# A decoder trunk's first mixer, its pieces put on TensorE in an order written out by hand

## The chip, the core and the metric

The kernel runs on one core of one Trainium2 chip. TensorE (PE in the profile) multiplies matrices and also transposes tiles by multiplying them with an identity. VectorE (DVE), ScalarE (ACT) and GpSimd (POOL) do the elementwise work, and SyncE (SP) issues most DMA transfers. Each engine takes its instructions in the order in which the program lists them for it. The metric is the device time of one execution in microseconds (us); less is better.

## What is computed

The trunk has two layers on 256 tokens of width 1024, all in float32. Each layer is a half-weighted SwiGLU block, a mixer, and another SwiGLU block. The change is in the first layer's mixer:

```python
z, xbc, dt, q_a, kv_a = split_last(h @ w_in, [SSM_D, SSM_XBC, SSM_HEADS, MLA_Q_RANK, MLA_KV_RANK + MLA_ROPE])
xbc = silu(causal_depthwise_conv(xbc, conv_w, conv_b))
xs, Bm, Cm = split_last(xbc, [SSM_D, SSM_GROUPS * SSM_STATE, SSM_GROUPS * SSM_STATE])
y = ssd_chunked(xs, softplus(dt + dt_bias), -exp(a_log), Bm, Cm) + d_skip * xs
y = rms_norm_by_group(y * silu(z), ssm_norm)
q = rms_norm(q_a, q_a_norm) @ w_q_b            # 8 heads of 96
kv = rms_norm(kv_c, kv_a_norm) @ w_kv_b        # 8 heads, keys 64 and values 64
o = causal_block_attention(norm_rope(q), norm_rope(k), v, 96 ** -0.5)
out = concatenate([y, o]) @ w_out
```

`ssd_chunked` is a state space scan in two chunks of 128 tokens: products of `C` and `B`, times decays `E`, applied to `x * dt`, and a state that goes from the first chunk to the second.

## The kernel before

Weights are read once, as tiles of 128 rows by up to 1024 columns (512 KB). `Stream.load` issues the DMA of a tile (`raw`, 4 buffers), ScalarE casts it to a rounded part `wh` (L77), and VectorE subtracts to get the rest `wl` (L78). `wh` and `wl` have 8 buffers each, used in turn, so that a cast must wait until TensorE is done with the tile that is 8 tiles older. Each product is three matmuls, with `wh` twice (high and low part of the activation) and with `wl` once.

`mixer0` computes in pieces. `in_tok` gives a piece with tokens on partitions: `qa` and `kva` (query and key ranks), and the gate `z` in four pieces (two halves of 512 columns by two token blocks, 24 matmuls of 512 columns each). `xbc(c)` gives one of 16 channel tiles (24 matmuls of 256 columns); `conv_silu` then runs on it: a ScalarE pass `cv`, three VectorE passes `cv`, a ScalarE tanh `cth` and a VectorE product into `xT` (tiles 0 to 7), `BT` (8 to 11) or `CT` (12 to 15). Four channel tiles are turned by TensorE transposes (`m_xsT`), after which VectorE makes `xd` and ScalarE `xs`. The attention has query and key pieces (`p_qb`, `p_kvb`), their turns (`m_qT`, `m_kT`), scores (`m_sc`), a softmax on VectorE, ScalarE and GpSimd, turned probabilities (`m_pT`) and the product with the values. The scan (`m_yd`) uses the decays `E`, which GpSimd loads from DRAM and ScalarE and VectorE work on.

TensorE's results go to PSUM banks in three groups: four of `bank` (`p_...`), and two each of the groups "a" and "b" of `sbank` (`m_...`). A piece can start only when a bank of its group has been read out.

The order in which the engines get their instructions is set by a planner. It takes the program in the order in which it is written, simulates a timeline, and moves instructions of one engine past each other as their inputs come ready. So in the kernel before the planner puts transposes and scores between matmuls of other pieces, sometimes one at a time. After the mixer's pieces comes the output product (`proj`), and then the next SwiGLU block.

## Time and profile before

| | |
|---|---|
| median of 3 executions | 1045.36 us (1044.97 to 1046.19) |
| the profiled execution | 1044.57 us, of which the span of the trace is 1042.8 us |
| mean granted TensorE clock | 0.995 |
| TensorE busy | 1017.3 us (98%) |
| VectorE busy | 686.2 us (66%) |
| ScalarE busy | 570.3 us (55%) |
| GpSimd busy | 87.5 us (8%) |
| the first mixer, from its first matmul to the next block's first | 197.48 to 376.77 us |

The profiled execution is one of its own and is 0.79 us below the median. Matmuls are pipelined, so that a busy TensorE is one with something in it; what a matmul costs is read from the distance between starts. A wait is shown with the instruction that ended it, the releaser.

### The profile page before, as it was taken

The page shows a single profiled execution, that of the slowest core. Times are in us where ns is not written, and L with a number is a line of the kernel's source. Part 1 is how long each engine was busy: PE and PEld are TensorE (multiplying, and loading weights), DVE is VectorE, ACT ScalarE, POOL GpSimd, SP SyncE. Part 2 cuts the span into 40 slices and gives each one's busy share as a digit, 9 for nine tenths or more (in the row PEclk, how much of TensorE's full clock was granted, in tenths as well). Part 3 has the DMA queues.
Part 4 walks back from the last instruction along what each step waited for, and adds up shares of the span by engine and source line. Part 5 has one row for each costly group of instructions (what it writes and reads, how often), then busy time and mean ns, then how long its engine had stood idle before and what let it go on. Part 6 is the DMA issues. An engine that isn't in the chain of part 4 may idle for free.

```text
span 1042.8 us, 15030 instructions
## 1 busy us (share of the span) xinstructions
PE 1017.3 (98%) x5561; PEld 872.3 (84%) x5561; DVE 686.2 (66%) x1054; ACT 570.3 (55%) x1036; POOL 87.5 (8%) x110
## 2 busy tenths in 40 slices
PE   6999999989799999999999999999999999999998
PEld 5888888988798888888888888888887778888886
DVE  6876754588777567677545767654588576666541
ACT  5755543467857366655434655643465456555530
POOL 2200000106233200000000000000011200000000
PEclk9999999999999999999999999999999999999999
DMA  8866555364434457565564655555463345665451
GB/s 300 280 204 188 191 190 176 115 209 162 151 111 161 144 182 241 184 198 184 197 190 159 223 197 186 191 189 168 142 222 101 102 160 181 191 193 184 148 197 40
DMA packets 52089, 185.93 MB, mean 178 GB/s; under 512 B 5911, under 2 KB 5928, under 8 KB 52016
## 3 DMA queue, kind: packets, MB, share of 16 engines
q1 hardware_dynamic: 49248, 176.58, 52.1%
q0 software_dynamic: 2048, 6.83, 2.0%
q10 hardware_dynamic: 720, 1.57, 0.4%
q8 instruction: 43, 0.70, 0.3%
q14 instruction: 30, 0.25, 0.1%
HBM read 183.89 MB, written 1.06 MB: 177 GB/s over the span
## 4 chain that ended last, share of the span: by engine, by line
PE 95%; ACT 1%; DVE 1%; DMA 1%; issue 1%; POOL 0%; DVEq 0%; ACTq 0%; POOLq 0%
PE p_u L300 13%; PE p_g L300 13%; PE p_acc L316 9%; PE p_acc L318 9%; PE p_acc L317 9%; PE p_u L301 7%; PE p_g L301 7%; PE p_g L272 1%; PE p_g L273 1%; PE p_g L274 1%; PE p_u L274 1%; PE p_u L272 1%; PE p_u L273 1%; PE p_xbc L289 1%; PE p_xbc L290 1%; PE p_xbc L291 1%
## 5 line engine op out<-in xcount | busy, mean ns | idle before, releaser
L78 DVE TENSOR_TENSOR wl<-raw,wh 128x1024 fp32r<-128x1024 f32 (+3 forms) x341 | 413.0, 1222 | 220.7 <-ACT wh L77 219.1
L77 ACT CAST wh<-raw 128x1024 fp32r<-128x1024 f32 (+3 forms) x341 | 351.8, 1038 | 306.1 <-PE p_acc L317 101.7
L300 PE MATMUL p_u<-hT,wh 128*128 128x512 f32 x576 | 204.1, 393 | 0.0
L300 PE MATMUL p_g<-hT,wh 128*128 128x512 f32 x576 | 204.0, 393 | 0.0
L301 PE MATMUL p_u<-hT,wl 128*128 128x256 f32 x576 | 161.7, 281 | 0.0
L301 PE MATMUL p_g<-hT,wl 128*128 128x256 f32 x576 | 161.5, 280 | 0.0
L318 PE MATMUL p_acc<-wl,acth 128*128 128x512 f32 x352 | 137.1, 389 | 0.0
L317 PE MATMUL p_acc<-wh,actl 128*128 128x512 f32 x352 | 137.0, 389 | 0.0
L316 PE MATMUL p_acc<-wh,acth 128*128 128x512 f32 x352 | 136.2, 391 | 0.0
L300 PEld LDWEIGHTS p_g<-hT,wh 128*128 128x128 f32 x576 | 107.9, 187 | 24.5
L300 PEld LDWEIGHTS p_u<-hT,wh 128*128 128x128 f32 x576 | 107.9, 187 | 24.4
L301 PEld LDWEIGHTS p_g<-hT,wl 128*128 128x128 f32 x576 | 108.9, 189 | 0.2
L301 PEld LDWEIGHTS p_u<-hT,wl 128*128 128x128 f32 x576 | 108.9, 189 | 0.0
L318 PEld LDWEIGHTS p_acc<-wl,acth 128*128 128x128 f32 x352 | 66.1, 188 | 13.8
L316 PEld LDWEIGHTS p_acc<-wh,acth 128*128 128x128 f32 x352 | 66.1, 188 | 13.6
L317 PEld LDWEIGHTS p_acc<-wh,actl 128*128 128x128 f32 x352 | 66.1, 188 | 13.4
L229 POOL TENSOR_TENSOR ss<-ss,mhalf 128x1 f32<-128x1 f32 x12 | 6.7, 557 | 577.5 <-DVE ss L247 577.5
L324 DVE SCALAR_TENSOR_TENSOR x<-p_acc,x 128x512 f32<-128x512 f32 x24 | 16.2, 688 | 36.4 <-PE p_acc L318 36.4
L289 PE MATMUL p_xbc<-hT,wh 128*128 128x256 f32 x128 | 38.2, 299 | 0.4 <-DVE cv L439 0.4
L290 PE MATMUL p_xbc<-hT,wh 128*128 128x256 f32 x128 | 37.8, 295 | 0.0
L291 PE MATMUL p_xbc<-hT,wl 128*128 128x256 f32 x128 | 37.6, 294 | 0.0
L376 DVE TENSOR_TENSOR sg<-sg 128x256 f32<-128x256 f32 x72 | 30.6, 426 | 7.9 <-DVE sg L373 0.9
(370 smaller groups left out, 1530.7 us busy)
## 6 DMA issues: line engine op xcount, KB each, us to landing
raw<-in_w SPq DMA_DIRECT2D x326, 512.0 KB, 4.3
gain<-in_gains POOLq DMA_DIRECT2D x5, 512.0 KB, 5.8
E<-acs_rows POOLq DMA_DIRECT2D x4, 512.0 KB, 6.2
raw<-in_w SPq DMA_DIRECT2D x4, 400.0 KB, 3.2
raw<-in_w SPq DMA_DIRECT2D x4, 288.0 KB, 2.8
raw<-in_w SPq DMA_DIRECT2D x3, 384.0 KB, 4.0
raw<-in_w SPq DMA_DIRECT2D x4, 272.0 KB, 2.9
out<-x ACTq DMA_DIRECT2D x4, 256.0 KB, 2.0
```

The costliest lines, as they stand in the source:

```text
L77: nc.scalar.copy(out=hi, in_=raw)
L78: nc.vector.tensor_tensor(out=lo, in0=raw, in1=hi.bitcast(F32), op=ALU.subtract)
L272: mm(out, ah, wh, start=first and i == 0, stop=False)
L289: mm(out, hi[:, cs], xh, start=k == 0, stop=False)
L290: mm(out, hi[:, cs], xl, start=False, stop=False)
L291: mm(out, lo[:, cs], xh, start=False, stop=k == KT - 1)
L300: mm(out, hi[:, cs], hT[k // 2][:, k % 2], start=k == 0, stop=k == KT - 1, skip_group_check=True)
L301: mm(out[:, 0, :], lo[:, cs], self.hk(hT, k)[0], start=False, stop=k == KT - 1, skip_group_check=True)
L316: first = nc.tensor.matmul(o, ah, w[0][:, s], start=k == 0, stop=False)
L317: nc.tensor.matmul(o, al, w[0][:, s], start=False, stop=False)
L318: nc.tensor.matmul(o, ah, w[1][:, s], start=False, stop=k == nk - 1)
L376: nc.vector.tensor_tensor(out=sg, in0=sg, in1=v[:, 1, :], op=ALU.mult)
```

## The change

Every TensorE instruction of the mixer from its start until the last two gated norms is chained to the one written before it (`put`, with `self.strict`), so that the planner keeps the written order on TensorE. The other engines' order is still the planner's. The mixer's code is cut into functions, which are called in the order that TensorE is to have. The first half of the gate (`z0`) comes before the query pieces, with its weights moved in the stream. Pieces that depend on each other have channel tiles between them. The load of `ssm_norm` goes from GpSimd's queue to SyncE's. Two pools of blocks grow by 2 and by 1 block, and the scratch for dynamic DMA shrinks to 8192. The instructions are the same ones, but for how many of them stand together.

```diff
+    def put(self, ins):
+        if self.strict:
+            if self.prev is not None:
+                self.order(ins, self.prev)
+            self.prev = ins
+        return ins
-    POOLS = {"a": (("a4", 4096, 9),), "b": (("b1", 1024, 2), ("b2", 2048, 4), ("b4", 4096, 13))}
+    POOLS = {"a": (("a4", 4096, 9),), "b": (("b1", 1024, 2), ("b2", 2048, 6), ("b4", 4096, 14))}
...
+        by_tokens(0)
+        by_tokens(1)
+        turn_tokens(0)
+        z0 = z(0)
+        z0(0)
+        turn_tokens(1)
+        z0(1)
...
+        query(0)
+        xbc(8, BC[0][:, 0, :])
+        query(1)
+        xbc(9, BC[0][:, 1, :])
+        turn_query(0)
+        key(0)
+        xbc(10, BC[0][:, 2, :])
+        turn_query(1)
+        key(1)
+        steps()
+        xbc(11, BC[0][:, 3, :])
+        turn_key(0)
+        xbc(12, BC[1][:, 0, :])
+        turn_key(1)
+        sums()
+        xbc(13, BC[1][:, 1, :])
+        scores(0, 0)
+        scores(0, 1)
+        rows = sums_by_rows()
+        xbc(14, BC[1][:, 2, :])
+        scores(1, 0)
+        scores(1, 1)
+        xbc(15, BC[1][:, 3, :])
+        turn_probs(0, 0)
+        scores(1, 2)
+        scores(1, 3)
...
+        for j in range(2):
+            xT[j] = self.blk([P, 4, S], "xT")
+            for i in range(4):
+                xbc(4 * j + i, xT[j][:, i, :])
+                if (j, i) == (0, 0):
+                    attend(0)
+                    products(0)
+                    decays(0, 0)
+                if (j, i) == (0, 1):
+                    turn_probs(1, 0)
+                    turn_probs(1, 1)
+                    decays(0, 1)
+                if (j, i) == (0, 2):
+                    attend(1)
+                if (j, i) == (1, 0):
+                    turn_x(0)
+                if (j, i) == (1, 1):
+                    scan(0, 0)
+                    products(1)
+                    decays(1, 0)
+        sn = self.blk([P, D], "ssmn", grp="a")
+        nc.sync.dma_start(out=sn, in_=self.args["ssm_norm"].partition_broadcast(P))
+        z1 = z(1)
+        z1(0)
+        turn_x(1)
+        gated(0, 0)
+        scan(1, 0)
+        scan(0, 1)
+        decays(1, 1)
+        turn_B()
+        turn_y(0, 0)
+        z1(1)
...
+        self.strict = False
-    nc = bacc.Bacc("TRN2", target_bir_lowering=False, num_devices=1)
+    nc = bacc.Bacc("TRN2", target_bir_lowering=False, num_devices=1, dynamic_dma_scratch_size=8192)
```

Where the change moves things is seen best at three places, each shown as the rows of an engine's list in the program. A row has the line, the operation, the output, the inputs and the engines that it waits for.

**The second key turn.** On TensorE before, the transposes of the keys of token block 1 (`m_kT`, from `knat`) stand in the middle of a channel tile's matmuls:

```order
L289 MATMUL p_xbc_276_2893<-hT2_40_222,wh49_0_2889 128x256
L290 MATMUL p_xbc_276_2893<-hT2_40_222,wh49_0_2889 128x256
L117 MATMUL m_kT_216_2521<-sq_79,knat_208_2483 96x128 [waits DVE_49,PE_49,Pool_49]
L117 MATMUL m_kT_216_2521<-sq_79,knat_208_2483 96x128 x3
L117 MATMUL m_kT_217_2527<-sq_79,knat_208_2483 96x128 [waits Activation_49]
L117 MATMUL m_kT_217_2527<-sq_79,knat_208_2483 96x128 x3
L291 MATMUL p_xbc_276_2893<-hT2_40_222,wl49_0_2890 128x256
```

In the changed kernel they stand behind the last matmul of channel tile 12 (weights `wh46_0` and `wl46_0`):

```order
L125 MATMUL p_xbc_223_2554<-hT3_41_223,wh46_0_2550 128x256 x2
L125 MATMUL p_xbc_223_2554<-hT3_41_223,wl46_0_2551 128x256
L125 MATMUL p_xbc_223_2554<-hT3_41_223,wh46_0_2550 128x256 x2
L125 MATMUL p_xbc_223_2554<-hT3_41_223,wl46_0_2551 128x256
L129 MATMUL m_kT_226_2587<-sq_79,knat_207_2441 96x128 [waits DVE_49,Activation_49,Pool_49]
L129 MATMUL m_kT_226_2587<-sq_79,knat_207_2441 96x128 x3
```

On ScalarE at this place the changed kernel has the cast of `wh54_0`, whose buffer was that of `wh46_0`, and the passes of tile 12 behind it:

```order
L77 CAST wh54_0_3087<-raw54_0_3085 128x1024 [waits DMAHW1_49,PE_49]
L449 ACTIVATE cv_224_2579<-p_xbc_223_2554,conv_17_140 128x256 [waits PE_49]
L454 ACTIVATE cth_220_2533<-cv_219_2528 128x256 [waits DVE_49,Activation_49]
L602 ACTIVATE kT1_171_2151<-m_kT_226_2587,kgain_22_151 96x512 [waits PE_49,Pool_49]
L454 ACTIVATE cth_225_2584<-cv_224_2579 128x256 [waits DVE_49,Activation_49]
```

On VectorE it has the subtraction for that weight tile, a pass of tile 12, and then the product that finishes `knat`:

```order
L78 TENSOR_TENSOR wl54_0_3088<-raw54_0_3085,wh54_0_3087 128x1024 [waits DMAHW1_49,PE_49,Activation_49]
L451 SCALAR_TENSOR_TENSOR cv_224_2579<-p_xbc_223_2554,conv_17_140,cv_224_2579 128x255 [waits Activation_49]
L593 TENSOR_TENSOR knat_207_2441<-knat_207_2441,rk_210_2449 128x8x64 [waits Pool_49]
L455 SCALAR_TENSOR_TENSOR BT_149_1921<-cth_220_2533,cv_219_2528 128x256 [waits Activation_49]
L451 SCALAR_TENSOR_TENSOR cv_224_2579<-p_xbc_223_2554,conv_17_140,cv_224_2579 128x254 [waits DVE_49]
```

The transposes moved from the inside of a piece to the end of one, and their input stands two VectorE instructions behind a weight tile whose buffer the piece just ended gives back.

**The first turn of channel tiles.** Before, on TensorE, the first transposes of tiles 0 to 3 (`m_xsT`) come one at a time, behind tile 4 (`p_xbc_287_3027`), with others from a softmax between:

```order
L290 MATMUL p_xbc_288_3027<-hT3_41_223,wh52_0_3023 128x256
L291 MATMUL p_xbc_288_3027<-hT3_41_223,wl52_0_3024 128x256
L117 MATMUL m_xsT_285_3004<-sq_79,xT_272_2847 128x128 [waits DVE_49]
L117 MATMUL m_xsT_286_3012<-sq_79,xT_272_2847 128x128 [waits PE_49]
L117 MATMUL m_pT_243_2681<-sq_79,p0_237_2649 128x128 [waits Pool_49]
L117 MATMUL m_pT_243_2681<-sq_79,p0_237_2649 128x128 x3
L289 MATMUL p_xbc_291_3066<-hT0_38_220,wh53_0_3062 128x256 [waits DVE_49]
L290 MATMUL p_xbc_291_3066<-hT0_38_220,wh53_0_3062 128x256
```

In the changed kernel all of them stand together behind tile 4 (weights `wh54_0`):

```order
L125 MATMUL p_xbc_290_3091<-hT3_41_223,wh54_0_3087 128x256 x2
L125 MATMUL p_xbc_290_3091<-hT3_41_223,wl54_0_3088 128x256
L129 MATMUL m_xsT_293_3124<-sq_79,xT_262_2830 128x128
L129 MATMUL m_xsT_293_3124<-sq_79,xT_262_2830 128x128 [waits DVE_49] x3
L129 MATMUL m_xsT_294_3132<-sq_79,xT_262_2830 128x128 x4
L125 MATMUL p_xbc_295_3146<-hT0_38_220,wh55_0_3142 128x256 x2
```

On VectorE the changed kernel has there the subtraction for the weight tile `wh60_0` (the buffer of `wh54_0`), passes of tiles 3 and 4, a product of the decays, and, last, the product that finishes tile 3 (`xT_262_2830`):

```order
L78 TENSOR_TENSOR wl60_0_3537<-raw60_0_3534,wh60_0_3536 128x1024 [waits DMAHW1_49,PE_49,Activation_49]
L451 SCALAR_TENSOR_TENSOR cv_291_3116<-p_xbc_290_3091,conv_17_140,cv_291_3116 128x255 [waits Activation_49]
L451 SCALAR_TENSOR_TENSOR cv_287_3076<-p_xbc_286_3051,conv_17_140,cv_287_3076 128x253 [waits DVE_49]
L698 TENSOR_TENSOR E01_280_2970<-E01_280_2970,cb_269_2887 128x512 [waits Pool_49]
L451 SCALAR_TENSOR_TENSOR cv_291_3116<-p_xbc_290_3091,conv_17_140,cv_291_3116 128x254 [waits DVE_49]
L455 SCALAR_TENSOR_TENSOR xT_262_2830<-cth_288_3081,cv_287_3076 128x256 [waits Activation_49]
```

**The second turn of channel tiles.** Before, on TensorE, the transposes of tiles 4 to 7 begin ahead of the third gate piece (`p_z`) and the rest of them come between its matmuls and the next piece's:

```order
L290 MATMUL p_xbc_297_3144<-hT3_41_223,wh55_0_3140 128x256
L291 MATMUL p_xbc_297_3144<-hT3_41_223,wl55_0_3141 128x256
L117 MATMUL m_xsT_300_3177<-sq_79,xT_287_3020 128x128 [waits Activation_49]
L117 MATMUL m_xsT_301_3185<-sq_79,xT_287_3020 128x128 [waits Activation_49]
L272 MATMUL p_z_308_3272<-wh56_0_3250,hT0_38_220 128x512
L273 MATMUL p_z_308_3272<-wh56_0_3250,hT0_38_220 128x512
L274 MATMUL p_z_308_3272<-wl56_0_3251,hT0_38_220 128x512
```

In the changed kernel they stand together behind the gate piece `z1(0)`, and the scans stand behind them:

```order
L125 MATMUL p_z_309_3314<-wh59_1_3310,hT3_41_223 128x512 x2
L125 MATMUL p_z_309_3314<-wl59_1_3311,hT3_41_223 128x512
L129 MATMUL m_xsT_311_3342<-sq_79,xT_289_3084 128x128 [waits DVE_49] x4
L129 MATMUL m_xsT_312_3350<-sq_79,xT_289_3084 128x128 [waits PE_49]
L129 MATMUL m_xsT_312_3350<-sq_79,xT_289_3084 128x128 x3
L125 MATMUL m_yd_315_3367<-xd1_261_2829,E10_301_3196 128x64 [waits DMASW5_49,Activation_49]
L125 MATMUL m_yd_315_3367<-xd1_261_2829,E10_301_3196 128x64 x7
```

On VectorE the gate product of that same piece (L528, from `p_z_309_3314`) stands ahead of the passes that finish tile 7 (`cv_306`, and `xT_289`), with `xd` and a product of the decays behind:

```order
L698 TENSOR_TENSOR E11_317_3387<-E11_317_3387,cb_300_3194 128x512 [waits DMASW6_49,Activation_49]
L451 SCALAR_TENSOR_TENSOR cv_306_3280<-p_xbc_305_3255,conv_17_140,cv_306_3280 128x254 [waits DVE_49]
L528 SCALAR_TENSOR_TENSOR gate_310_3339<-gate_310_3339,p_z_309_3314 128x512 [waits Activation_49]
L451 SCALAR_TENSOR_TENSOR cv_306_3280<-p_xbc_305_3255,conv_17_140,cv_306_3280 128x253 [waits DVE_49]
L455 SCALAR_TENSOR_TENSOR xT_289_3084<-cth_307_3285,cv_306_3280 128x256 [waits Activation_49]
L711 TENSOR_TENSOR xd0_260_2828<-m_xsT_311_3342,dts_1914 128x512 [waits PE_49]
L698 TENSOR_TENSOR E11_317_3387<-E11_317_3387,cb_300_3194 128x512 [waits Activation_49]
L711 TENSOR_TENSOR xd1_261_2829<-m_xsT_312_3350,dts_1914 128x512 [waits PE_49]
```

So here as well the transposes moved to the end of a piece, and on VectorE their input stands behind an instruction that needs that piece.

## Rows read from the trace of the kernel before

**Rows 1.** The page: TensorE's busy time, and the chain that ended last.

```profile
PE 1017.3 (98%) x5561; PEld 872.3 (84%) x5561; DVE 686.2 (66%) x1054; ACT 570.3 (55%) x1036; POOL 87.5 (8%) x110
PE 95%; ACT 1%; DVE 1%; DMA 1%; issue 1%; POOL 0%; DVEq 0%; ACTq 0%; POOLq 0%
```

**Rows 2.** TensorE's waits from 197 to 377 us: total, times, longest.

```profile
PE m_pT L117 <- POOL p L415: 5.3, 1, 5.3
PE m_qaT L117 <- DVE qn L483: 3.3, 1, 3.3
PE p_kvb L272 <- ACT qr L524: 0.7, 1, 0.7
...
PE p_xbc L289 <- DVE cv L439: 0.4, 1, 0.4
```

**Rows 3.** Windows: busy us of PE, PEld, DVE, ACT, POOL; granted clock; DMA.

```profile
219.90:223.20 3.30, 0.01 (x1) 0.04 (x1) 2.80 (x5) 3.30 (x5) 0.00 (x0) 1.00 0.67 220
223.60:226.90 3.30, 3.30 (x18) 3.30 (x17) 3.30 (x6) 0.80 (x3) 0.00 (x0) 0.50 0.68 227
240.00:260.00 20.00, 18.22 (x129) 16.31 (x128) 17.01 (x42) 15.36 (x35) 12.19 (x18) 1.00 0.55 183
281.60:288.40 6.80, 4.25 (x18) 3.85 (x19) 6.80 (x13) 4.07 (x13) 2.97 (x2) 0.50 0.33 108
290.00:330.00 40.00, 40.00 (x285) 35.27 (x284) 29.48 (x53) 26.02 (x60) 13.01 (x13) 1.00 0.39 132
```

**Rows 4.** TensorE's timeline: two channel-tile matmuls, then two gate matmuls (start, duration).

```profile
276.04 0.28 PE L290 MATMUL p_xbc<-hT,wh 128*128 128x256 f32 x1
276.16 0.28 PE L291 MATMUL p_xbc<-hT,wl 128*128 128x256 f32 x1
...
314.04 0.39 PE L272 MATMUL p_z<-wh,hT 128*128 128x512 f32 x1
314.27 0.39 PE L273 MATMUL p_z<-wh,hT 128*128 128x512 f32 x1
```

**Rows 5.** ScalarE's timeline: start, duration, instruction, idle time before it.

```profile
257.42 1.05 ACT L77 CAST wh<-raw 128x1024 fp32r<-128x1024 f32 x1
...
260.01 1.05 ACT L77 CAST wh<-raw 128x1024 fp32r<-128x1024 f32 x1 [1.07 <-PE p_xbc L290]
260.97 0.56 ACT L437 ACTIVATE cv<-p_xbc,conv 128x256 f32<-128x256 f32 x1
265.49 2.16 ACT L649 ACTIVATE E<-E,acs 128x128 f32<-128x128 f32 x7 [3.96 <-DMA E<-acs_rows]
...
268.94 0.72 ACT L442 ACTIVATE cth<-cv 128x256 f32<-128x256 f32 x2
...
327.29 1.05 ACT L701 ACTIVATE gate<-p_z 128x512 f32<-128x512 f32 x2
```

**Rows 6.** VectorE's timeline, the same columns.

```profile
258.51 1.23 DVE L78 TENSOR_TENSOR wl<-raw,wh 128x1024 fp32r<-128x1024 f32 x1 [1.33 <-ACT wh L77]
259.65 0.48 DVE L439 SCALAR_TENSOR_TENSOR cv<-p_xbc,conv,cv 128x255 f32<-128x255 f32 x1
260.04 1.02 DVE L558 TENSOR_TENSOR knat<-knat,rk 128x512 f32<-128x512 f32 x1
260.98 0.47 DVE L439 SCALAR_TENSOR_TENSOR cv<-p_xbc,conv,cv 128x254 f32<-128x254 f32 x1
...
277.27 0.42 DVE L443 SCALAR_TENSOR_TENSOR xT<-cth,cv 128x256 f32<-128x256 f32 x1
...
281.18 1.29 DVE L655 TENSOR_TENSOR E<-E,cb 128x512 f32<-128x512 f32 x2
...
328.02 1.28 DVE L702 SCALAR_TENSOR_TENSOR gate<-gate,p_z 128x512 f32<-128x512 f32 x2
```

**Rows 7.** VectorE by line, 200 to 375 us: the product `xd`.

```profile
L679 DVE TENSOR_TENSOR xd<-m_xsT,dts 128x512 f32<-128x512 f32 x4 | 2.7, 688 | 1.0 <-ACT xs L678 1.0
```

**Rows 8.** The page's DMA issues: the decays' load, to its landing.

```profile
E<-acs_rows POOLq DMA_DIRECT2D x4, 512.0 KB, 6.2
```

More of the change, by code (lines that the diff above doesn't have):

```diff
@@ L500, in xbc, with query @@
             self.in_ch(b, hT, w)
[L501 to L511 removed]
+            self.conv_silu(c, b, out)
+        sq = self.small([P, 2, 8], "sqs")
+        qnat, knat, wq, wkv = {}, {}, [], []
+        def query(t):
+            if not t:
+                wq.extend(st.load([768, 768]) + st.load([768]))
+            c = half(t)
+            qn = qnat[t] = self.blk([P, 8, 96], "qnat", grp="a")
             qr = self.blk([P, 8, 2, 16], "qr")
@@ new lines, in steps @@
+        def steps():
+            e = self.small([P, 2, 16], "dte")
+            l1 = self.log1p_exp(dtv, e, "dtl")
+            nc.vector.scalar_tensor_tensor(out=dts, in0=dtv, scalar=0.0, in1=l1, op0=ALU.max, op1=ALU.add)
+            ea = self.small([P, 16], "ea")
+            nc.scalar.activation(out=ea, in_=row[:, ROW["a_log"]], func=AF.Exp)
+            nc.vector.scalar_tensor_tensor(out=a.rearrange("p (t h) -> p t h", t=2), in0=dts, scalar=-1.0,
+                                           in1=ea.unsqueeze(1).broadcast_to([P, 2, 16]), op0=ALU.mult, op1=ALU.mult)
@@ new lines, in sums, with sums_by_rows @@
+        def sums():
+            ba = self.sbank([P, 32], "acs")
+            mm(ba, u, a, start=True, stop=True)
+            nc.vector.tensor_copy(out=acs, in_=ba)
+            nc.scalar.activation(out=eacs, in_=acs[:, 16:], func=AF.Exp)
+        def sums_by_rows():
+            bt = self.sbank([32, P], "acsT")
+            self.transpose(bt, acs)
+            at_ = self.blk([32, P], "acsT")
+            nc.scalar.copy(out=at_, in_=bt)
+            rows = self.tc.dram_tile([32, P], F32, name="acs_rows")
+            nc.gpsimd.dma_start(out=rows, in_=at_)
+            return rows
@@ L635, in decays, with products @@
+        def products(t):
+            c = half(t)
             b = self.sbank([P, 4, P], "CB")
@@ L691, in mixer0 @@
-        scan(0, E0)
-        E1 = decays(1)
-        gate = {}
-        for j in range(2):
-            wz = [s for _ in range(2) for s in st.load([D, D])]
-            for t in range(2):
-                b = self.bank([P, 512], "z")
-                self.in_tok(b, hT, t, wz, 512, 2)
-                g = gate[t, j] = self.blk([P, 512], "gate")
-                nc.scalar.activation(out=g, in_=b, func=AF.Tanh, scale=0.5)
-                nc.vector.scalar_tensor_tensor(out=g, in0=g, scalar=1.0, in1=b, op0=ALU.add, op1=ALU.mult)
@@ L729, in mixer0, with scan @@
-        gated_norm(0)
-        Bn = self.blk([P, 4, P], "Bn")
-        tp = self.tbank([P, 4, P], "Bn", "b")
-        for g in range(4):
-            self.transpose(tp[:, g, :], BC[0][:, g, :P])
-        nc.scalar.copy(out=Bn, in_=tp)
-        state = self.blk([P, D], "state")
-        cols = [(slice(512 * j, 512 * j + 512), slice(8 * j, 8 * j + 8)) for j in range(2)]
-        for j, (s, hs) in enumerate(cols):
+        def scan(t, j):
+            s = slice(512 * j, 512 * j + 512)
+            b = self.sbank([P, 8, 64], "yd")
+            for i in range(8):
+                h = 8 * j + i
+                mm(b[:, i, :], E[t, j][:, i, :], xd[t][:, 64 * h:64 * h + 64], start=True, stop=True)
+            nc.vector.tensor_tensor(out=xs[t][:, s], in0=b.rearrange("p a b -> p (a b)"), in1=xs[t][:, s], op=ALU.add)
@@ L750, in mixer0, with gated @@
             nc.gpsimd.tensor_tensor(out=xs[1][:, s], in0=xs[1][:, s], in1=off, op=ALU.add)
-        scan(1, E1)
-        gated_norm(1)
+        yT = {}
+        def gated(t, j):
+            y = xs[t]
+            s = slice(512 * j, 512 * j + 512)
+            nc.vector.scalar_tensor_tensor(out=y[:, s], in0=y[:, s], scalar=0.5, in1=gate[t, j], op0=ALU.mult, op1=ALU.mult)
+            ss = self.small([P, 2], "ssy", bufs=2)
+            rs = self.small([P, 2], "rsy", bufs=2)
+            for i in range(2):
+                g = slice(512 * j + 256 * i, 512 * j + 256 * i + 256)
+                nc.scalar.activation(out=gate[t, j][:, :256], in_=y[:, g], func=AF.Square, scale=1.0 / 16, accum_out=ss[:, i:i + 1])
+            nc.vector.tensor_scalar(out=ss, in0=ss, scalar1=EPS, scalar2=None, op0=ALU.add)
+            self.power(rs, ss)
+            for i in range(2):
+                g = slice(512 * j + 256 * i, 512 * j + 256 * i + 256)
+                nc.vector.scalar_tensor_tensor(out=y[:, g], in0=y[:, g], scalar=rs[:, i:i + 1], in1=sn[:, g], op0=ALU.mult, op1=ALU.mult)
@@ new lines, in mixer0 @@
+        turn_key(0)
[13 more added lines that the diff above has]
+        scores(1, 3)
+        xs = [self.blk([P, D], f"xs{t}") for t in range(2)]
+        xd = [self.blk([P, D], f"xd{t}") for t in range(2)]
@@ new lines, in mixer0 @@
+        sn = self.blk([P, D], "ssmn", grp="a")
[10 more added lines that the diff above has]
+        z1(1)
+        gated(0, 1)
+        states(0)
+        states(1)
+        turn_y(0, 1)
+        from_states(0)
+        from_states(1)
+        scan(1, 1)
+        self.strict = False
@@ L755, in at @@
+        for j in range(2):
+            gated(1, j)
+            turn_y(1, j)
         def at(k, t):
```

276 lines of the change are left out of this document (122 added, 154 removed).

## The prediction

> **What bounds the kernel now.** I read the page's busy times and the chain that ended last first [rows 1]: TensorE is busy in 98% of the span and makes up 95% of the chain, so only time in which TensorE stops, or runs at a lower clock, can be won or lost. The other engines matter where they make it stop. The change touches the first mixer alone, so I read TensorE's waits there next [rows 2]. Six kinds make 10.8 us in all: two long ones, 5.3 us ahead of turned probabilities and 3.3 us ahead of the turned ranks, and four short ones of 0.4 to 0.7 us. Then the windows [rows 3], for the granted clock. After the 3.3 us stop it is 0.50 for 3.3 us of work (half of 2.4 GHz), after the 5.3 us stop it is 0.50 in a window with 4.25 us of work. At half clock half of such work is lost: 1.65 and 2.1 us. The reader is to see in these rows that everything which this mixer loses is 10.8 + 1.65 + 2.1 = 14.6 us, and that a better order can't win more.
>
> One more balance decides much. A channel tile costs TensorE 24 matmuls at 0.12 us from start to start [rows 4], 2.88 us. It costs VectorE one subtraction (1.14 us from its start to the next), three passes (0.39 each) and a product (0.42) [rows 6], 2.73 us. So in a row of channel tiles VectorE has almost nothing to spare for scores, decays or copies. A gate piece costs TensorE 24 x 0.227 = 5.45 us [rows 4], and VectorE little: in the stretch where all four gate pieces lay, TensorE didn't stop once in 40 us while VectorE worked 29.5 [rows 3].
>
> **The change part by part.** *What it removes.* The 3.3 us stop came because the ranks' turn had no work ahead of it. Now 5.45 us of gate stand between. I don't take it for gone, since casts and subtractions for the query weights stand ahead of the ranks on ScalarE and VectorE; it counts below among the short waits. The 5.3 us stop came from a softmax right ahead of its turn; a channel tile now stands between, and it too becomes a short one. With them the clock's 1.65 and 2.1 us go.
>
> *What it adds: three turns behind the end of a piece.* On TensorE nothing can pass a waiting instruction, and the order now has three places where the input of a turn can't be ready, by the order of the other engines.
>
> At the second key turn, the last input `knat` stands on VectorE behind the subtraction for `wl54_0`. Its cast needs the buffer of `wh46_0`, which TensorE reads until the end of tile 12, the piece just ahead of the turn. So from the end of tile 12 to the turn there lie a cast, a subtraction, a pass and the key product. Before has this very chain: the cast starts at 257.42 [rows 5], the subtraction at 258.51, the pass at 259.65, the product at 260.04, for 1.02 [rows 6]. That is 3.64 us.
>
> At the first turn of channel tiles, the same tie: the cast of `wh60_0` needs the buffer of tile 4, and tile 4 stands right ahead of the turn. Behind its subtraction VectorE has two passes, a decay product, a pass and the product for tile 3. With 1.09 from the cast's start to the subtraction's [rows 5, 6], 1.14, three passes of 0.39, 0.645 for a decay product (two took 1.29) and 0.42 [rows 6] this makes 4.47 us.
>
> At the second turn of channel tiles, the gate's own tanh (0.525, two took 1.05) and product (0.64, two took 1.28) stand ahead of the last pass of tile 7 (0.39), the tanh of that tile (0.36, two took 0.72) and its product (0.42) [rows 5, 6]: 2.34 us after the gate piece ends. The scan behind it needs VectorE's two `xd` (0.69 each [rows 7]) with a decay product of 0.645 between, 2.02 us, of which four transposes at 0.12 cover 0.48: 1.5 us more. Together the three places cost 3.64 + 4.47 + 2.34 + 1.5 = 12.0 us. Before, these turns were split up between other matmuls, and TensorE's waits show none of over 0.4 us at any of them [rows 2].
>
> *The decays' loads.* They are issued later than before, one by one, and take 6.2 us to land [rows 8]. ScalarE's list has their first pass ahead of casts and of the tanh that the second turn needs. Before, ScalarE stood 3.96 us at such a load [rows 5] while TensorE had enough ahead. Here the last loads are issued around the first turn, about two channel tiles and a gate piece ahead of the second. The cost for TensorE is between 0 and 3.96 us; I take 1.5, nearer to nothing, since 11.2 us of tensor work stand between.
>
> *Short waits.* Five places keep an ordinary risk: the ranks' turn, the two scores behind tile 14 (whose banks an exponential must free), and the turned probabilities of each token block. The nearest rows are the short waits of 0.4 to 0.7 us [rows 2]. I take 0.7 each, 3.5 us. The bounds are nothing, and a cast with its subtraction, 1.09 + 1.14 = 2.2 us, each: 11 us.
>
> *The clock.* Two of the new stops are as long as those after which it fell, and the third is near if the decays come late. I take 1.7 and 1.9 us (between the 1.65 and 2.1 of rows 3) and half of 1.7 for the third: 4.4 us. The bounds are 0 and three times 2.1, 6.3. Short stops are another matter: between 240 and 260 us TensorE was busy in 18.22 of 20 us, with several stops of under a microsecond, and the clock stayed at 1.00 [rows 3]. The Trainium skill says in "TensorE: Matmul & The Clock Gate", section "A second HAM failure mode: psum-queue depth-cycling", that frequent micro-idles between groups of matmuls made the clock swing between its two states in another kernel. By that rule the five short waits would each cost a spell at half clock too, five times 1.65, 8.3 us, and the sum would come out near 1060. The trace speaks against it at the number of short stops that before has.
>
> *What costs nothing.* The `ssm_norm` load now stands on SyncE ahead of weight tiles that only the output product reads, behind a gate piece of 5.45 us; if it held them up it would cost at most that product's first tile, a cast and a subtraction of 2.2 us. More blocks and the smaller scratch add no instruction. They can only take waits away, which the stops above don't wait for.
>
> *The sum.* After: 12.0 + 1.5 + 3.5 + 4.4 = 21.4 us lost. Before: 14.6. The profiled execution of 1044.57 us becomes 1051.4. The median shown is 0.8 above that execution, so I say 1052.2 us. With every bound low the loss is 12.0 us, 2.6 less than now, a median of 1042.8; with every bound high it is 12.0 + 4.0 + 11 + 6.3 = 33.3, 18.7 more, 1064.
>
> **The rivals.** *A faster kernel.* The written order puts one or two tiles between dependent pieces, so that every turn comes to TensorE with its input ready. For it: both long stops of before are ended by such a distance. Against it: the two ties through the weight buffers and the gate product ahead of tile 7 leave a distance of nothing at three places. Price: if these four waits too are short ones, 0.6 us each, the loss is 2.4 + 3.5 us with no half clock, 5.9, so 8.7 less than now: 1036.7 us. It decides as soon as stops and clock together stay below 14.6 us. What could bring it about is VectorE and ScalarE being far ahead with all but the tied instructions, so that the chains are shorter than read.
>
> *No change.* The change doesn't do what it says: it trades two long stops and their half clock for three others of the same kind. For it: low short waits and a clock that falls only once, 12.0 + 1.5 + 1.0 = 14.5. It gives 1043.3 to 1047.5.
>
> *Decays in the way.* ScalarE stands at the decays' loads, and all behind it, casts too, comes late: the second turn waits its 2.34 + 3.96, the clock falls three times, 6.3, and short waits double to 7: 12.0 + 4.0 + 7 + 6.3 = 29.3, which is 14.7 more, 1060. For it: before, ScalarE lost 3.96 us at one load [rows 5], and VectorE has no spare time in channel tiles to catch up. Against it: every long stop lets the others catch up. The skill's rule above would end near the same time, and is counted here.
>
> **How the numbers follow.** My forecast, 1047.5 to 1056, gets 0.47; the rival with the decays, above 1056, 0.20; no change 0.13; faster 0.20. The likeliest one's own range is 1047.5 to 1056. 0.2% (2.1 us) is about what a measurement of this kernel can tell from no change. So slower has 0.67. The range goes from 1042, which leaves out the better part of the faster cases (0.13), to 1062, above which some 0.06 is left.
>
> **What the profile would show.** Right: TensorE waits of 2 to 5 us for VectorE at the second `m_kT` and at both `m_xsT` turns, with ScalarE's cast ended by a TensorE channel tile just ahead, and granted clocks of 0.50 behind them; the waits at `m_qaT` and `m_pT` small; TensorE's work in the mixer otherwise equal. Wrong: if these turns show waits of under a microsecond, the chains that I counted from the end of the piece ran earlier; if a wait of over 2 us stands at a place that I call short, the balance of VectorE or a decay load is what I mis-sized; if the time outside the mixer moves, the change reaches further than its rows.

## The result, and the profile after

The changed kernel is slower: 1061.97 us in the median of four (1060.77 to 1065.28) against 1045.16, a ratio of 1.0167 with an interval of 1.0150 to 1.0185. The direction was forecast. That the time lies inside the range, by 0.03 us, is luck: it is above the 1047.5 to 1056 of the likeliest case, and the loss is 16.8 us where 6.8 were forecast.

The page of the profiled execution (1065.28 us, with a span of 1063.5, the slowest of the four) answers to [rows 1] with a lower share of TensorE in the chain, and has the granted clock below 0.9 in the four slices from 266 to 372 us:

```profile
PE 1027.8 (97%) x5561; PEld 881.3 (83%) x5561; DVE 685.9 (64%) x1054; ACT 572.1 (54%) x1036; POOL 83.3 (8%) x109
PEclk9999999999888899999999999999999999999999
...
PE 93%; DVE 3%; ACT 2%; DMA 1%; issue 1%; POOL 0%; ACTq 0%; POOLq 0%
```

TensorE's waits from 195 to 400 us, to be held against [rows 2]:

```profile
PE m_xsT L129 <- DVE xT L455: 10.9, 4, 3.9
PE m_kT L129 <- DVE knat L593: 3.4, 1, 3.4
PE m_qaT L129 <- DVE qaTl L237: 2.7, 1, 2.7
PE m_sc L125 <- ACT p L658: 1.1, 2, 0.7
PE m_sc L125 <- DVE pT L438: 0.9, 1, 0.9
PE m_pT L129 <- POOL p L427: 0.8, 1, 0.8
PE m_pT L129 <- DVE pT L438: 0.8, 1, 0.8
PE m_yd L125 <- ACT xs L712: 0.5, 1, 0.5
```

These add up to 21.1 us, 10.3 more than before. The 10.9 us at the turns of channel tiles (x turns below) are four stops, two at each turn:

```profile
311.60 0.33 PE L129 MATMUL m_xsT<-sq,xT 128*128 128x128 f32 x1 [2.20 <-DVE xT L455]
315.83 1.33 PE L129 MATMUL m_xsT<-sq,xT 128*128 128x128 f32 x5 [3.90 <-DVE xT L455]
...
337.22 0.33 PE L129 MATMUL m_xsT<-sq,xT 128*128 128x128 f32 x1 [2.21 <-DVE xT L455]
340.17 1.33 PE L129 MATMUL m_xsT<-sq,xT 128*128 128x128 f32 x5 [2.62 <-DVE xT L455]
```

The other half is the clock. Below, a stop is such a wait of TensorE, and a spell is a stretch in which the granted clock is at half. Windows over the five spells (columns as in [rows 3]):

```profile
223.60:226.90 3.30, 3.30 (x9) 2.53 (x9) 1.69 (x3) 1.06 (x2) 0.00 (x0) 0.51 0.30 114
261.20:267.90 6.70, 5.58 (x27) 5.55 (x28) 2.71 (x7) 1.78 (x4) 0.67 (x2) 0.51 0.37 121
285.10:288.40 3.30, 3.30 (x17) 3.14 (x17) 2.57 (x8) 1.62 (x5) 0.00 (x0) 0.52 0.54 163
312.40:319.10 6.70, 3.27 (x16) 3.27 (x17) 5.39 (x11) 2.37 (x5) 1.56 (x2) 0.51 0.41 141
339.70:353.20 13.50, 12.48 (x52) 11.53 (x53) 5.35 (x9) 4.22 (x11) 3.52 (x4) 0.50 0.01 4
```

TensorE worked 27.9 us in them, which costs 14.0 us, against 3.8 before (7.55 us of work in the two spells of [rows 3]). So 10.3 us of stops and 10.2 of clock make 20.5 of the 20.7 us between the two spans.

The other three executions are 2.2 to 4.5 us shorter, at a mean granted clock of 0.986 to 0.988 where this one has 0.984. In the median the clock thus cost nearer 10 than 14 us. This is an estimate: the 16.8 us between the medians and the 14.6 lost before make 31.4, of which 21.1 are stops, if these are the same in every execution.

The mixer as a whole (first matmul of `qa` to the next block's first matmul) shows the same sum, 200.2 us for 179.3 before; behind it the two executions both take 666 us. Here is the window for the changed kernel, and under it that for the first experiment:

```profile
197.40:397.60 200.20, 179.07 (x1100) 162.49 (x1099) 134.61 (x237) 118.96 (x259) 46.86 (x59) 0.91 0.42 140
```

```profile
197.30:365.90 168.60, 164.54 (x1101) 150.48 (x1100) 138.97 (x238) 116.65 (x260) 45.72 (x59) 1.00 0.50 168
```

### The profile page after: what moved, and what is told of

The parts are those of the page before. It is cut to its first block, busy times and chain, and to the rows that moved or that the text cites. A ratio compares the mean times of both kernels' runs of the same rounds, so it can differ in the third digit from the quotient of the medians.

```text
span 1063.5 us, 14972 instructions
## 1 busy us (share of the span) xinstructions
PE 1027.8 (97%) x5561; PEld 881.3 (83%) x5561; DVE 685.9 (64%) x1054; ACT 572.1 (54%) x1036; POOL 83.3 (8%) x109
## 4 chain that ended last, share of the span: by engine, by line
PE 93%; DVE 3%; ACT 2%; DMA 1%; issue 1%; POOL 0%; ACTq 0%; POOLq 0%
PE p_g L125 23%; PE p_u L125 23%; PE p_acc L328 9%; PE p_acc L330 9%; PE p_acc L329 9%; PE p_xbc L125 3%; PE p_tok L125 2%; PE p_z L125 2%; PE m_nrm L129 1%; PE m_yd L125 1%; PE p_q L125 1%; DVE wl L78 1%; PE p_qa L125 1%; DVE cv L451 1%; PE m_sc L950 1%
## 5 line engine op out<-in xcount | busy, mean ns | idle before, releaser
L125 PE MATMUL p_xbc<-hT,wh 128*128 128x256 f32 x256 | 50.7, 299 | 0.0
L125 PE MATMUL p_g<-wh,hT 128*128 128x512 f32 x128 | 44.6, 406 | 0.0
L125 PEld LDWEIGHTS p_xbc<-hT,wh 128*128 128x128 f32 x256 | 43.0, 204 | 0.6 <-issue 0.2
L125 PE MATMUL p_u<-wh,hT 128*128 128x512 f32 x128 | 42.5, 392 | 0.0
```

What stands on the lines that cost most here:

```text
L125: return self.put(self.nc.tensor.matmul(*args, **kwargs))
```

## The experiments

In the table, stops are TensorE's waits in the mixer, and half clock the length of the spells at 0.50 there, both in the profiled execution, whose own time can lie some us off the median. Of the kernel before these are 10.8 and 10.2 us, of the changed one 21.1 and 34.1.

| run | median us | ratio to before, interval | stops | half clock |
|---|---|---|---|---|
| e1 planner's order | 1034.34 | 0.9900 (0.9885 to 0.9915) | 4.0 | 0 |
| e2 stops filled | 1066.75 | 1.0207 (1.0183 to 1.0231) | 9.2 | 6.8 |
| e3 gate back | 1061.65 | 1.0157 (1.0137 to 1.0176) | 19.5 | 30.7 |
| e4 scans later | 1060.33 | 1.0154 (1.0136 to 1.0173) | 20.9 | 20.5 |
| e5 later turns | 1049.03 | 1.0044 (1.0029 to 1.0059) | 12.8 | 10.2 |
| e6 blocks only | 1044.75 | 1.0000 (0.9987 to 1.0013) | 10.5 | 13.7 |
| e7 nine buffers | 1063.97 | 1.0181 (1.0164 to 1.0198) | 22.9 | 34.1 |
| e8 free late | 1041.80 | 0.9974 (0.9960 to 0.9989) | 7.4 | 6.8 |
| e9 free early | 1057.83 | 1.0122 (1.0103 to 1.0142) | 14.5 | 34.1 |
| e10 planner, gate back | 1040.25 | 0.9958 (0.9944 to 0.9973) | 8.5 | 6.8 |
| e11 gate only | 1042.06 | 0.9974 (0.9956 to 0.9992) | 7.8 | 6.8 |
| e12 untied | 1057.87 | 1.0117 (1.0085 to 1.0148) | 19.3 | 23.9 |
| e13 no decay work | 1055.35 | 1.0096 (1.0067 to 1.0125) | 14.7 | 10.2 |
| e14 untied, no decay work | 1053.88 | 1.0077 (1.0050 to 1.0105) | 14.7 | 20.5 |

**e1: the planner's order, all else of the change.**

```diff
-        self.strict, self.prev = True, None
+        self.strict, self.prev = False, None
```

> Theory A, the written order is the cause: it puts three turns right behind the piece whose end their inputs wait for. With the order on TensorE left to the planner again, and all else of the change kept (gate half up front, new grouping of the weights, more blocks, smaller scratch), the stops at the second key turn (3.4 us) and at the two turns of channel tiles (6.1 and 4.8 us) should shrink to under 1 us each, and the time go to 1042 to 1050 us. Theory B, the gate half up front is the cause, since it takes cover away from the stretch of channel tiles: the time stays above 1055 us.

Without the written order the changed kernel is 27.6 us faster, and beats the kernel before by 11.1 us, which is below the range named: I had expected no gain from the rest of the change. The 27.6 us include what the planner then does differently on the other engines, since it makes their order for the one that it has on TensorE. TensorE's waits in the mixer are down to these, none of them at a turn of keys or channel tiles:

```profile
PE m_pT L129 <- issue: 1.8, 1, 1.8
PE p_acc L328 <- ACT yT L236: 1.7, 1, 1.7
PE p_z L125 <- DVE cv L451: 0.3, 1, 0.3
PE p_acc L329 <- DVE yT L237: 0.2, 1, 0.2
```

Theory A stands as far as the order goes; theory B falls.

**e2: the stops filled with work.**

```diff
+        def fill(tp, n, rows=P):
+            x = self.hk(hT, 0)[0]
+            o = tp.rearrange("p a b -> p (a b)")
+            for _ in range(n):
+                mm(o[:, :256], x[:, :rows], x, start=True, stop=True)
...
+            if t:
+                fill(tq, 22)
+                if (t, j) == (1, 0):
+                    fill(tp, 28, 96)
+                if not t:
+                    fill(tp, (50, 42)[j])
```

> Matmuls without use (128x256, into the bank that the turn then overwrites) are put ahead of four turns: 22 at the second ranks' turn, 28 at the second key turn, 50 and 42 at the turns of channel tiles, about as long as the stops there. They shorten no chain. Theory A with half of the loss in the clock (27.9 us of work at half clock, 14 us lost): the stops vanish from the list of waits, the half-clock spells but for one of 3.4 us vanish too, and the time falls by about 12 us to 1050. If the stops alone are the loss and the clock's spells cost little, the time stays at 1060 or goes up.

The time missed: 1066.75 is what the other theory named. The profile shows why that theory doesn't hold all the same. The clock did come back, to one spell of 6.8 us, but the fills cost more than the stops that they took the place of. At the ranks' turn the wait is for a bank, which the fill too must wait for, so its 2.9 us came on top; at the x turns a stop of 0.7 to 0.8 us each stayed behind the fill, and the scan's wait grew from 0.5 to 1.7. Stops of 9.2 and fills of 17.7 us are 5.8 more than 21.1; the mixer in the profile is still 5.3 us shorter, so some 11 us came back from the clock. Outside the mixer this execution is 3.6 us longer than the changed kernel's, which isn't explained, and it is the shortest of its four: the others, at a granted clock of 0.992 to 0.993 for 0.996, had about twice the time at half clock. As a cure the fills are no use.

**e3: the gate half back, order written.**

```diff
-        z0 = z(0)
-        z0(0)
         turn_tokens(1)
-        z0(1)
...
                 if (j, i) == (1, 0):
+                    z0 = z(0)
+                    z0(0)
                     turn_x(0)
+                    z0(1)
```

> The written order is kept, but the first gate half stands where before had it, around the first turn of channel tiles: one piece between tile 4 and the turn, one behind the turn. Theory A: the stop there (6.1 us) and its half clock go, the ranks' turn gets a stop of 3 us or more, the key turn and the second turn stay as they are: 1052 to 1058 us. Theory B: VectorE and ScalarE catch up in all of the stretch behind, the second turn's stop halves too, and the time falls to 1045 to 1051 us.

```profile
311.19 0.77 PE L129 MATMUL m_xsT<-sq,xT 128*128 128x128 f32 x5 [1.81 <-DVE xT L455]
...
335.53 0.33 PE L129 MATMUL m_xsT<-sq,xT 128*128 128x128 f32 x1 [1.12 <-DVE xT L455]
337.89 1.33 PE L129 MATMUL m_xsT<-sq,xT 128*128 128x128 f32 x5 [2.02 <-DVE xT L455]
```

The first x turn's stop fell from 6.1 to 1.8 us, with no half clock behind it, and the ranks' turn got one of 6.5 us where it had 2.7. The key turn kept its 3.4 us. The second x turn has 3.1 us for 4.8, less than the half that theory B named. The time is 3.7 us above what theory A said, and far from B's.

**e6: the blocks and the scratch alone,** put into the kernel before.

```diff
-    POOLS = {"a": (("a4", 4096, 9),), "b": (("b1", 1024, 2), ("b2", 2048, 4), ("b4", 4096, 13))}
+    POOLS = {"a": (("a4", 4096, 9),), "b": (("b1", 1024, 2), ("b2", 2048, 6), ("b4", 4096, 14))}
```

> The kernel before with only the larger pools (6 and 14 blocks) and the smaller scratch. Both theories: no wait of TensorE hangs on them, 1045 us give or take 2. If the smaller scratch slowed GpSimd's DMA issues, the decays' loads would take more than 6.2 us to land and the time would go up by 3 us or more.

They cost and give nothing.

**e5: three turns one piece later.**

```diff
-        turn_key(1)
         sums()
         xbc(13, BC[1][:, 1, :])
+        turn_key(1)
...
-                if (j, i) == (1, 0):
+                if (j, i) == (1, 1):
                     turn_x(0)
-                if (j, i) == (1, 1):
+                if (j, i) == (1, 2):
                     scan(0, 0)
...
         z1(0)
-        turn_x(1)
         gated(0, 0)
+        z1(1)
+        turn_x(1)
```

> The written order is kept, but three turns come one piece later: the second key turn behind tile 13, the first turn of channel tiles behind tile 5 (its scan one tile later), the second one behind the second piece of z1, with the scans last. Theory A (a turn right behind the piece whose end its inputs wait for): at the key turn the chain of 3.4 us now lies beside a tile of 2.88 us, a stop of about 0.5 us; at the second turn of channel tiles beside 5.45 us, none; at the first one the planner again has put VectorE work for the newest tile ahead of tile 3's product, so a stop of 3 to 4 us stays. With the half clocks behind the first two the time falls to 1043 to 1049 us. Theory B (VectorE and ScalarE are overloaded wherever the turns stand): the stops move with the turns, 1057 us or more.

```profile
PE m_xsT L129 <- DVE xT L455: 5.1, 2, 4.8
...
PE m_kT L129 <- DVE knat L593: 0.3, 1, 0.3
```

As expected, a piece between is enough at the key turn (0.3 us left) and at the second x turn (none); 4.8 us stay at the first, where 3 to 4 were expected. So the distance was the fault at two of the three places. Of the 12.9 us gained a part comes of the scans, which here stand behind the second gate piece, as in e4.

**e7: nine weight buffers.**

```diff
-        self.st = Stream(self.nc, wp, args["w"], 4, 8)
+        self.st = Stream(self.nc, wp, args["w"], 4, 9)
```

> Nine weight buffers where there were eight, and the two pools of blocks as before the change. If the stop at the second key turn came of too few buffers, it goes with one tile more to work ahead, and with it a part of the first x turn's: 1050 to 1056 us. Theory A, by the order of the rows: the planner runs one tile further ahead and puts the next subtraction, again for a buffer that tile 12 gives back, at the same place ahead of the key product; the stop stays at 3.4 us, and the time at 1059 to 1064 us.

The key turn's stop is 3.7 us: the planner used the ninth buffer to run a tile further ahead, and the next subtraction took the old one's place ahead of the key product. The x turns' stops grew, to 6.7 and 5.9 us.

**e8 and e9: one half of the order written.** `self.strict` is set to False behind the last scores (e8), or to True only there (e9).

```diff
         scores(1, 3)
+        self.strict = False
```

> The written order holds up to the last scores only; from the first x tile on the planner orders TensorE. Theory A, with the sums of the trace by stage: from there on the changed kernel stops for 11.5 us and works 15.8 us at half clock (7.9 lost), 19 us in all, which should go: 1042 to 1047 us. If the earlier part is what delays the later one, less is won: over 1050 us.

> The other half: the planner orders TensorE up to the last scores, and the written order holds from the first x tile on. Theory A, with the sums of the trace: up to there the changed kernel stops for 9.7 us and loses 6.1 us to the clock; freeing it wins most of this, 1046 to 1051 us, while the two x turns keep their stops of 6.1 and 4.8 us. If the late stops came of an early delay, they shrink too, and the time falls below 1044 us.

e8 came out as the sums by stage said, 20.2 us less than the changed kernel where 19 were expected. e9 missed: 1057.83. TensorE now waits for ScalarE's exponentials at the scores and at the first attention product:

```profile
PE m_xsT L129 <- DVE xT L455: 6.8, 3, 3.1
PE m_sc L125 <- ACT p L658: 3.2, 1, 3.2
PE m_att_o L125 <- ACT p L658: 1.8, 1, 1.8
```

A spell at half clock of 20.5 us begins within the first of these two stops. Freeing the late half gains 20.2 us and freeing the early half 4.1, where the sums by stage had 15.8 for it; so the early half's loss doesn't go by itself. My reading is that the x tiles, chained from there on, are no longer there as cover for the scores ahead of them. No run tries this apart.

**e10 and e11: where the 11 us come from.** e10 is e3 with the planner's order. e11 is the kernel before with the gate half up front (and the blocks of e6).

```diff
+        z(0)
         BC = [self.blk([P, 4, S], n) for n in ("BT", "CT")]
```

> The planner's order on TensorE as in the run that had it (1034 us), but with the first gate half back around the first x turn. If the gate half up front is what makes that run 11 us faster than the kernel before, by covering the ranks' turn, this one has a stop of 3 us there again, with its half clock, and takes 1038 to 1046 us. If the new grouping of weights and pieces does it, it stays at 1033 to 1036 us.

> The kernel before, code and planner's order, with only the gate half up front (and the blocks and scratch of the change, which alone gave 1044.75 us). If the cover at the ranks' turn is the half of the gain that the gate brings, its stop of 3.3 us goes with its half clock, and the stop of 5.3 us at the turned probabilities stays: 1039 to 1043 us. If the gate half is missed where it stood, among the late pieces, the time stays at 1045 us or goes up.

Both came out inside the first ranges named. Each has one of the two long stops left, here e10's and then e11's:

```profile
PE p_qb L125 <- ACT qaTh L236: 7.0, 1, 7.0
```

```profile
PE m_pT L117 <- POOL p L415: 5.4, 1, 5.4
```

The gate half up front takes away the first, the new grouping of pieces the second, and e1 has neither of the two stops. Against the kernel before, e10 gains 4.4 and e11 2.9 us, 7.3 of the 11.1; e10's stop is 3.7 us longer than the one that it stands for, which is about the rest.

**e4: the scans behind the second gate piece.**

```diff
         turn_x(1)
         gated(0, 0)
+        z1(1)
         scan(1, 0)
         scan(0, 1)
```

> In the changed kernel the clock stays at half for 13.65 us behind the second x turn, while TensorE works on 32 scan products of 64 columns, eight transposes and the first gate matmuls. Here the second piece of z1 stands between that turn and the scans. If the scans are what keeps the clock down, the spell ends after 3.4 or 6.8 us, which gives back 3.4 to 5.1 us, and with the 0.5 us stop the time falls to 1056 to 1059 us. If the length of the stop alone decides, the spell stays at about 13.65 us and the time at 1061 us or more.

The spell is 3.4 us long, as the scans' theory said, and the 32 scan products, which took 7.09 us in the changed kernel, take half. The 0.55 us stop ahead of the scans went too, and the run doesn't part the two. First the changed kernel's row, then e4's:

```profile
342.04 7.09 PE L125 MATMUL m_yd<-xd,E 128*128 128x64 f32 x32 [0.55 <-ACT xs L712]
```

```profile
347.50 3.68 PE L125 MATMUL m_yd<-xd,E 128*128 128x64 f32 x32
```

The median fell by 1.6 us only, and 1060.33 is above the range named; between the two profiled executions it is 5.0 us, but the changed kernel's is the longest of its four. In e4's profile the spell at 285 us is 6.8 us long where the changed kernel's was 3.4, so the spells behind short stops differ between executions.

**e12: TensorE's order kept, the three ties undone** by order edges on VectorE and ScalarE. A tie is an instruction that needs the end of the piece just ahead of a turn, and stands on its engine ahead of the turn's last input.

```diff
+                st.hold[54, 0] = (None, turned)
+                behind[12] = turned
...
+                    st.hold[60, 0] = last[3]
+                    behind[4] = last[3][1]
...
+                if (t, j) == (0, 1):
+                    self.order(th, last[7][0])
+                    self.order(pr, last[7][1])
```

(`hold` puts a weight tile's cast and subtraction behind the two instructions given, `behind` a channel tile's first VectorE pass.)

> TensorE's written order is kept row for row; only the order of VectorE and ScalarE is changed at the three turns: the subtraction for the weight tile, and the first pass of the newest channel tile, come behind the product that the turn waits for (key product; product of tile 3, with the cast behind its tanh), and the tanh and product of the gate piece behind those of tile 7. No instruction is added or taken away. Theory A, the ties at the three turns are the cause: the key turn's stop falls from 3.4 to under 0.5 us, the first x turn's from 6.1 to 1 or 2 us (ScalarE still has its pass of tile 4 ahead of the tanh), the second one's from 4.8 to 1 to 3 us, the half clocks behind them go or get short, and the time falls to 1041 to 1048 us. Theory B, VectorE and ScalarE have too much to do in this stretch whatever their order: the stops stay or move, and the time stays above 1054 us.

This missed: theory A falls as far as the ties go, and the time is theory B's. Only 4.1 us were gained. The second x turn's stop fell from 4.8 to 2.9 us, as expected, while the scan's wait behind it grew from 0.5 to 1.7; the stops at the other two turns stayed:

```profile
PE m_xsT L133 <- DVE xT L461: 8.2, 3, 5.3
PE m_kT L133 <- POOL knat L608: 2.9, 1, 2.9
PE m_yd L129 <- ACT xs L726: 1.7, 1, 1.7
```

At the key turn GpSimd's half of the key product now comes last, nearly as late. Tile 12's matmuls end there at 259.7, and GpSimd's timeline goes on from that:

```profile
259.71 1.64 POOL L245 TENSOR_TENSOR rk<-rk,mhalf 128x8 f32<-128x8 f32 x1 [5.45 <-PE p_xbc L129]
261.43 1.12 POOL L608 TENSOR_TENSOR knat<-pr,rk 128x256 f32<-128x256 f32 x1
```

The scale `rk` of the keys takes GpSimd 1.64 us, and both halves of the key product need it. VectorE's half, freed of the tie, starts 1.7 us behind the tile's end, for 2.5 in the changed kernel. So the tie was worth under a microsecond here.

At the first x turn ScalarE is late, in the changed kernel too. Its timeline there (start, duration):

```profile
306.17 2.45 ACT L692 ACTIVATE E<-E,acs 128x128 f32<-128x128 f32 x8
308.51 1.05 ACT L77 CAST wh<-raw 128x1024 fp32r<-128x1024 f32 x1
309.45 0.57 ACT L449 ACTIVATE cv<-p_xbc,conv 128x256 f32<-128x256 f32 x1
309.91 0.41 ACT L454 ACTIVATE cth<-cv 128x256 f32<-128x256 f32 x1
...
314.55 0.42 ACT L454 ACTIVATE cth<-cv 128x256 f32<-128x256 f32 x1 [1.78 <-DVE cv L451]
```

Tile 4's matmuls end at 309.0. Eight passes on the decays (L692) stand ahead of the cast, the pass `cv` of tile 3 and the tanh of tile 2 (309.91). The turn's last tanh starts at 314.55, after waiting 1.78 us for a pass of VectorE, so both engines are in this path.

**e13 and e14: ScalarE's work on the decays left out,** from the changed kernel and from e12.

```diff
-                for i in range(4):
-                    first = nc.scalar.activation(out=eb[:, i, :], in_=eb[:, i, :], func=AF.Relu, scale=-1.0, bias=acs[:, h:h + 1])
...
-                nc.scalar.activation(out=eb, in_=eb, func=AF.Exp, scale=-1.0)
```

> The changed kernel without ScalarE's work on the decays (32 passes of 128x128 and 8 exponentials are left out, so the scan's values are not the real ones); the loads and VectorE's products stay. Theory L, the decay work stands on ScalarE ahead of the tanh that each x turn needs and is what the stops there are longer by than the ties: the first x turn's stop falls from 6.1 us to the tie's 3 us, the second's from 4.8 to 1.5 or 2 us, the key turn's stays at 3.4: 1047 to 1053 us. Theory T, the ties alone make the stops: they stay within 1 us of what they were, 1058 us or more.

> The same work left out of the untied kernel. With tie and decay work both gone, theory L has under 1 us left at the first x turn (5.3 with the decay work) and under 1 us at the second; the key turn, which now waits for GpSimd, stays at 2.9 us: 1041 to 1047 us. If the stops stay above 2 us here too, VectorE's load in a row of channel tiles is the cause and neither theory holds.

The stops at the first x turn are 6.1 us in the changed kernel, 5.3 untied, 2.55 without the decay work, 1.55 with neither; at the second (without the scan's wait) 4.8, 2.9, 1.7 and 1.6. So the decay work makes 3.5 to 3.7 us of the first and the tie 0.8 to 1.0. At the second it makes 3.2 with the tie and 1.3 without, and the tie 1.9 with the decay work and next to nothing without. Leaving the work out takes away ScalarE's waits at the decays' loads too, 3.3 us in the changed kernel, all of them between the two turns; so at the first turn it is the work, and at the second the run doesn't part the two. What makes the 1.6 us that stay isn't shown. e13's stops came out as theory L said; its time is 2.4 us above the range named. e14 misses in both: 1.6 us stayed at each x turn, and the time is 6.9 us above the range. e14 also shows what the clock does behind shorter stops:

```profile
330.10 0.33 PE L133 MATMUL m_xsT<-sq,xT 128*128 128x128 f32 x1 [0.58 <-DVE xT L461]
331.45 0.77 PE L133 MATMUL m_xsT<-sq,xT 128*128 128x128 f32 x5 [1.03 <-DVE xT L461]
333.42 7.09 PE L129 MATMUL m_yd<-xd,E 128*128 128x64 f32 x32 [1.20 <-ACT xs L720]
```

```profile
332.70:342.70 10.00, 9.28 (x42) 9.18 (x43) 2.92 (x5) 2.12 (x5) 3.09 (x3) 0.50 0.00 0
```

Three stops of 0.6 to 1.2 us with a few transposes between, and TensorE is at half clock for 10 us, of which the scans take 7.1.

## Why the prediction was right in direction and wrong in size

**The clock is the step that failed.** The sum had 4.4 us for it, with 6.3 as its upper bound; it is 14.0 in the profiled execution, and about 10 in the median. Two readings were wrong.

First, I took only stops of more than 2 us to bring the clock down, from two such cases in [rows 3]. The ranks' turn, which I counted as a short wait, stopped for 2.7 us and brought a spell. The spell at 285 us follows stops of 0.7, 0.4, 0.8 and 0.9 us, and e14's follows the three above. The Trainium skill ("TensorE: Matmul & The Clock Gate", "A second HAM failure mode: psum-queue depth-cycling") says that frequent micro-idles between groups of matmuls made the clock swing in another kernel. That agrees with these rows, and my case against it, the 20 us at full clock of [rows 3] with three stops of 0.5 to 0.7 us, didn't carry over. But the same four stops stand in e2 and e13, and there the clock stayed at full. Here is e13's window over them:

```profile
271.00:290.00 19.00, 16.21 (x136) 14.75 (x135) 12.61 (x30) 14.19 (x43) 7.30 (x8) 1.00 0.20 69
```

So such stops can bring the clock down, and don't always.

Second, I took a spell's length from spells that had channel tiles in them. Behind the second x turn TensorE went into scans, and the spell had 12.5 us of work, 6.2 us lost where I had 0.85; with a gate piece there instead it ended after 3.4 us (e4).

**The stops** were 17.0 in the sum and are 21.1. The key turn is 3.39 for 3.64. The second x turn is 4.83 for 2.34 and the 1.5 of the decays; the scan behind it 0.55 for 1.5. The short waits but for the ranks' turn are 3.6 for 2.8. Two places were mis-sized. The first x turn is 6.1 for 4.47: of the decays I had counted only ScalarE's waits at their loads, and only for the second turn; its work on them, which the sum has at nothing, stood ahead of the first (e13). The waits at the loads got shorter. Here is ScalarE's wait for them from 200 to 375 us, before and after:

```profile
ACT E L649 <- DMA E<-acs_rows: 8.1, 2, 4.2
```

```profile
ACT E L692 <- DMA E<-acs_rows: 3.3, 2, 2.1
```

The ranks' turn, which I counted at 0.7 with 2.2 as its bound, is 2.7: it waits for the copies that empty the previous turn's two banks (`qaTl`, `kvT`), which ScalarE and VectorE do late, behind casts and subtractions for the query weights as I had feared. The gate piece ahead of it covers a part: without it the stop is 6.5 us (e3).

**The chains** were right in length at the key turn, and not as the only cause there. At the key turn and the first x turn the tie through the weight buffer that I followed is one of several paths that end within about a microsecond of each other, so untying it moved little (e12). What they share is what the forecast said: the written order brings TensorE to a turn too soon for its inputs. e5 shows that at the key turn and the second x turn a piece of distance is enough. The cost of the blocks, the scratch and the `ssm_norm` load at nothing held for the first two (e6); the load was not tried apart, but the output product has no wait in the changed kernel's list above.

**The rival of a faster kernel** was right in that both long stops could be taken away, and wrong in that the written order would do it: e10 and e11 each take away one of them, and e1, with both gone under the planner's order, gains 11.1 us.

**The rival with the decays in the way** had 1060, and the time fell there. Its mechanism, ScalarE standing at the loads, is not what the trace shows (3.3 us of such waits for 8.1 before). Its price had 6.3 us for the clock and 23.0 for the stops; measured are 14.0 and 21.1.

The changed code also does a little more than its description says, and "the other engines' order is still the planner's" isn't quite so. At each of the four decay loads ScalarE's first pass is ordered behind the newest tanh, where before only the first one was. Some copies out of banks were swapped: ranks are copied out behind both turns, and `xd` is made ahead of `xs`. e1 has all of this as well, and no run takes it alone.

Not settled: how much of the 1.6 us left at each x turn in e14 is VectorE's load and how much the pace of single passes; and why spells behind short stops come in some executions and not in others.

## What to carry to other kernels

An order written out for the engine that bounds the kernel must leave, ahead of each dependent piece, as much other work as the longest of all the paths into it, on every engine: write down the two or three latest inputs, not the latest one. Before keeping such an order, run the same code with the planner's: here the regrouping gained 11 us and the order lost 28. And where short stops stand close together, or thin work follows a stop, count the clock as well.

## What the runs showed of the hardware

The granted clock had two levels, 1.00 and 0.50 (2.4 and 1.2 GHz), and at the lower one the same 32 scan products took 7.09 us for 3.68.

With the scans behind the second x turn, a spell at half clock lasted 13.65 us in the changed kernel, e3 and e9, 17.1 in e7, 10.2 in e12 and e14, and 6.8 in e13. With matmuls of 512 columns there it lasted 3.4 us (e4, one execution).

Stops of 0.6 to 1.2 us were enough to bring the clock down in e14, where transposes and scans stood between and behind them. Before, three stops of 0.5 to 0.7 us among channel tiles left it at 1.00, and so did single stops of 1.8 and 1.7 us in e1. At the ranks' turn stops of 2.3 to 2.5 us (e2, e8, e13) left it at 1.00 too, and stops of 2.7 to 3.3 us (before, the changed kernel, e4 to e6, e12, e14) were each followed by 0.50. These are single executions, and no rule is drawn from them.
